# A two-layer retention and block-attention trunk: a load behind a transpose counted later, and a rotation's last steps ranked lower

## The chip, the core and the metric

The kernel runs on one core of a Trainium2 chip. Five engines work side by side, each through its own list of instructions in order: TensorE (PE, matrix products), VectorE (DVE), ScalarE (ACT), GpSimd (POOL) and SyncE (SP). In this kernel SP issues nearly all DMAs. The metric is the time of one execution on the device in microseconds (us), lower is better.

## What is computed

The reference, cut to its body. `D_MODEL` is 1024, there are 256 positions, two layers, four retention heads and four attention heads of 128 columns each.

```python
for i in range(DEPTH):
    h = rms_norm(x, norm_g[i])
    proj = h @ w_in[i]
    rq, rk, rv, rz, mq, mk, mv, mz = jnp.split(proj, cuts, axis=-1)
    r_out = retention(rotary(heads(rq, RET_HEADS), pos), rotary(heads(rk, RET_HEADS), pos),
                      heads(rv, RET_HEADS), ret_norm_g[i])
    r_out = jax.nn.silu(rz.astype(f32)) * r_out
    q_m = rms_norm(heads(mq, MOBA_HEADS), q_norm_g[i])
    k_m = rms_norm(heads(mk, MOBA_HEADS), k_norm_g[i])
    m_out = moba(q_m, k_m, heads(mv, MOBA_HEADS), rel_bias)
    m_out = jax.nn.silu(mz.astype(f32)) * m_out
    y = jnp.concatenate([r_out, m_out], axis=-1).astype(x.dtype) @ w_out[i]
    x = x + y
    gate = jax.nn.sigmoid((rms_norm(x) @ w_ple_gate[i]).astype(f32))
    e = rms_norm(p[i] @ w_ple[i], ple_norm_g[i]).astype(f32)
    x = x + (gate * e).astype(x.dtype)
```

With 256 positions there is one attention block, so `moba` is causal softmax attention with a bias by distance. `retention` is a decayed product of queries and keys times values, in two chunks of 128, with a norm per head. `rotary` turns pairs of columns: `x1*cos - x2*sin` and `x1*sin + x2*cos`.

## The kernel before

**Products in three parts.** Each float32 matrix is split into a high part (a copy rounded to the type that PE multiplies) and a low part (the rest). A product is three matmuls into one PSUM bank: high times high, high times low, low times high (`mm3`, lines 358, 359 and 360). The 256 positions are two halves m of 128 rows.

**Weights.** They come in 96 pieces of 0.5 MB (`Stage`). Each piece is one load by SP into a buffer `wst` (line 314, eight buffers), a rounding copy on ACT into `wh` (line 319), and a subtraction on DVE into `wl` (line 321). In the second half of each layer some pieces go to buffers lent by other tiles and are called T, V, PS or G in the rows. I count the pieces from 1 in the order of their loads. PE uses one piece for twelve matmuls as a rule.

**Stages of a layer.** The input projection runs by groups of 512 columns: MQ, MK, RQ, RK, MZ, MV, RV, RZ (M for attention, R for retention; queries, keys, values and gate). Then follow the output projection, a small product for the per-layer embedding, and its gate. Each result in PSUM (`acc`, four banks) is read by a chain of small steps on the other engines:

- MQ and MK: a norm (`qk_norm`).
- RQ and RK: the rotation (`rope`), for each m a product with cosines (line 732, into `tmp`), a product with sines (line 734, into `tok`; after it the bank is free), and their sum (line 737).
- All of these, the softmax probabilities and the inputs of the next product then have to be turned, since PE needs them the other way round. ACT copies the 16-bit halves apart (`halves`, line 520, into `u`), SP issues a DMA transpose (`turned`, line 530, `w<-u`), and DVE copies the halves together again (line 539, two copies each).

Two short groups of PE work stand between the projections: the attention scores (line 820) and, later, the probabilities times values (line 831), and the same for retention (lines 882 and 831).

**What sets the order.** The program is put in order while it is written, by a planner in the kernel (`Flow`). PE's work is written out by hand. Every other step is part of a chain (a Python generator) that asks for an engine and a cost (`ask`). Each time PE's clock moves on, the planner takes the engine that can start first, and among the chains that can start on it then, the one with the smallest key; a key is about the time by which PE needs the chain. `lay` advances the clocks. For DMAs the planner keeps one more clock, `dma`: a load adds 2.5 us per MB (3.3 at first), a transpose 1.4 us. `can` holds back a DMA whose start lies far ahead of that clock, and a load that isn't urgent if a transpose would soon be ready. On the chip nothing of these clocks is left: the engines keep the order and wait on semaphores.

The key of a rotation is PE's clock plus 4 (RQ) or 2 (RK) when its bank is full, and holds for the whole chain, from the first product to the last turned copy. The key of a piece of weights is its due time less 7, so it moves up as PE nears it.

Of the kernel before, what the change touches and what calls it, by code (L numbers as in the profile page):

```python
# [60 lines left out]
class Chain:  # L61
# [3 lines left out]
    def __init__(self, gen, key, at):  # L65
        self.gen, self.key, self.ready, self.done, self.on = gen, key, at, False, None
        self.next()
# [14 lines left out]
class Flow:  # L82
# [4 lines left out]
    def __init__(self, slots):  # L87
        self.clock = {PE: 0.0, ACT: 3.0, DVE: 1.0, POOL: 1.0, SP: 0.7}
        self.dma = 0.0
        self.live = []  # L90
        self.free_at = {k: [0.0] * n for k, n in slots.items()}
        self.lent, self.lending = [], False
        self.loaded = 0.0
        self.end = 0.0

    def begin(self, gen, key, at=None):
# [53 lines left out]
    def lay(self, start, c):  # L150
        eng, cost, take, after, mb = c.want
        for s in take:
            t = min(self.free_at[s])
            self.free_at[s].remove(t)
            self.got = None
            for i, (at, names) in enumerate(self.lent):
                if s == "w" and at == t:
                    self.got = self.lent.pop(i)[1]
                    break
        if eng == POOL and start - self.clock[POOL] > 1.5:  # L160
            cost += 0.9
        self.end = self.clock[eng] = start + cost
        c.ready, c.on = self.end, eng
        if mb is not None:
            rate = 3.3 if self.dma < 11 else 2.5
            self.dma = max(self.dma, start + (1.3 if mb else 1.0)) + (rate * mb if mb else 1.4)
            c.ready = self.dma + (0.9 if mb else 0.65)
            if mb:
                self.loaded = start
            else:  # L170
                c.ready += 0.75 * max(0.0, self.loaded + 2.6 - start)
        c.next()
        if c.done:
            self.live.remove(c)
# [57 lines left out]
def ask(eng, cost, take=(), after=(), mb=None):  # L232
    return eng, cost, take, after, mb
# [3 lines left out]
def tile_hybrid_trunk(ctx: ExitStack, tc: tile.TileContext, first, rest, x, pT, ple_g, rel_bias,  # L237
# [278 lines left out]
    def halves(src, name):  # L516

        yield ask(ACT, 0.95, take=("u16",))
        u = tok_p.tile([P, 2, GW], U16, name="u16", bufs=U_BUFS)
        nc.scalar.copy(u, src.bitcast(U16).rearrange("p (n t) -> p t n", t=2))  # L520
        if name:
            flow.free(name)
        return u
# [151 lines left out]
    def layer(l, aT):  # L675
        last = l == DEPTH - 1
        T, TC, V, G, VC, GC = {}, {}, {}, {}, {}, {}
# [7 lines left out]
        def to_heads(name, m, u, scale=None):  # L685

            def raw():
                if name not in T:
                    T[name] = big.tile([P, H, S], F32, name="T")
                return T[name].bitcast(U16).rearrange("p h (k t) -> p t h k", t=2)[:, :, :, m * P:(m + 1) * P]  # L690
            yield from turned(u, raw, () if m else ("T",))
            if scale is not None:
                dst = T[name][:, :, m * P:(m + 1) * P]
                yield ask(ACT, 0.64)
                nc.scalar.activation(dst, dst, AF.Copy, scale=scale)
# [26 lines left out]
        def rope(g, m, ps):  # L722


            src = ps.rearrange("p (h a d) -> p h a d", h=H, a=2)
            cos, sin = (rot[:, m, j].rearrange("p (a d) -> p a d", a=2)[:, None].to_broadcast([P, H, 2, DH // 2])
                        for j in range(2))
            yield ask(DVE, 0.605, take=("tmp", "tok"), after=(L_ROT,))
            t = tmp_p.tile([P, GW], F32, name="tmp")
            o = tok_p.tile([P, GW], F32, name="tok")  # L730
            tv, ov = (v.rearrange("p (h a d) -> p h a d", h=H, a=2) for v in (t, o))
            nc.vector.tensor_tensor(tv, src, cos, op=ALU.mult)
            yield ask(DVE, 0.605)
            nc.vector.tensor_tensor(ov, src[:, :, ::-1], sin, op=ALU.mult)  # L734
            flow.free("acc")
            yield ask(DVE, 0.605)
            nc.vector.tensor_tensor(o, o, t, op=ALU.add)
            flow.free("tmp")
            u = yield from halves(o, "tok")
            yield from to_heads(g, m, u)  # L740
# [19 lines left out]
        def after_proj(g, m, ps):  # L760
            fn, slack = {MQ: (qk_norm, -3 if l else 2), MK: (qk_norm, -3 if l else 0), RQ: (rope, 4), RK: (rope, 2), MZ: (gate, 4),
                         MV: (value, 1), RV: (value, -4), RZ: (gate, -4)}[g]
            c = flow.begin(fn(g, m, ps), flow.soon(slack))
            {MV: VC, RV: VC, MZ: GC, RZ: GC}.get(g, TC)[g, m] = c
            if g == RZ:
                YC[m, 0] = made(yT, m, 0, flow.begin(ret_gate(m), flow.soon(-5)))
# [397 lines left out]
```

## Time and profile before

| | |
|---|---|
| time, median of three runs | 308.04 us (307.85, 308.04, 311.3) |
| the profiled execution, first to last instruction (span) | 305.8 us |
| DVE busy | 251.1 us (82%) |
| ACT busy | 210.1 us (69%) |
| POOL busy | 33.8 us (11%) |
| the 96 subtractions of line 321, of which 83 into `wl` | 99.6 us for the 83, 1218 ns each |
| the 40 + 32 + 12 copies of line 539 | 16.3 + 12.6 + 4.8 us, about 455 ns each |
| mean granted TensorE clock | 0.997 |

The profiled execution has its span, and no time of its own beside it: the median of the runs lies 2.2 us above the span, for what lies before the first and after the last instruction. In the rows, "128x512" is partitions by elements, "x4" a count, and in brackets stands how long the engine was idle before the row and what ended that. Rows of a timeline begin with start and duration in us; instructions of one engine overlap a little, so the pace is taken from start to start.

### The profile page before, as it was taken

To read this page: it belongs to the slowest core of one execution; us is meant where nothing else is said; L and a number is where in the kernel's file an instruction comes from. 1 tells how busy PE (TensorE), PEld (TensorE's weight loads), DVE (VectorE), ACT (ScalarE), POOL (GpSimd) and SP (SyncE) were. 2 spreads that over 40 slices of the span, in tenths; PEclk is the share of its full clock that TensorE was granted. 3 is DMA by queue.
4 is the path that set the end of the run, shared out by engine and by line. 5 is a ranking of instruction groups with operands and counts; after the bars stand their busy time and mean duration, and the time that the engine had idled before them with its cause. 6 is when DMAs were issued, how large, how long until landed. Compare 5 with 4: busy or idle time off the path is not lost.

```text
span 305.8 us, 4251 instructions
## 1 busy us (share of the span) xinstructions
PE 298.7 (98%) x1393; PEld 248.8 (81%) x1393; DVE 251.1 (82%) x463; ACT 210.1 (69%) x359; POOL 33.8 (11%) x44
## 2 busy tenths in 40 slices
PE   8999999979999999999999999999999999999994
PEld 4888888868888888888888888888888888888884
DVE  4986899799787798799998578999868779959832
ACT  4976949885455975997694795797445678499211
POOL 6005200000002200121002220000000130012000
PEclk9999999999999999999999999999999999999998
DMA  7998999999579868795879669678976956833011
GB/s 252 406 408 302 286 290 278 274 273 353 220 145 375 270 175 275 166 230 223 214 230 266 219 171 270 146 172 190 383 287 135 339 195 192 241 75 64 0 71 69
DMA packets 61773, 69.76 MB, mean 228 GB/s; under 512 B 46260, under 2 KB 47032, under 8 KB 61624
## 3 DMA queue, kind: packets, MB, share of 16 engines
q1 hardware_dynamic: 61712, 69.50, 76.5%
q8 instruction: 11, 0.18, 0.2%
q14 instruction: 10, 0.08, 0.1%
q0 software_dynamic: 32, 0.01, 0.0%
q10 hardware_dynamic: 8, 0.00, 0.0%
HBM read 57.42 MB, written 1.05 MB: 191 GB/s over the span
## 4 chain that ended last, share of the span: by engine, by line
PE 89%; DVE 5%; DMA 2%; issue 1%; ACT 1%; DVEq 0%; ACTq 0%
PE acc L359 25%; PE acc L360 25%; PE acc L358 25%; PE acc L454 4%; PE mix L831 4%; DVE wl L321 2%; DMA w<-u 2%; PE mix L273 1%; PE mix L651 1%; PE mix L649 1%; PE mix L650 1%; PE mix L882 1%; ACT tok L802 1%; PE mix L820 1%; DVE tok L734 1%
## 5 line engine op out<-in xcount | busy, mean ns | idle before, releaser
L359 PE MATMUL acc<-wl,a 128*128 128x512 f32 (+1 forms) x332 | 127.6, 384 | 1.6 <-DVE wl L321 1.6
L358 PE MATMUL acc<-wh,a 128*128 128x512 f32 (+1 forms) x332 | 128.4, 387 | 0.0
L360 PE MATMUL acc<-wh,a 128*128 128x512 f32 (+1 forms) x332 | 127.5, 384 | 0.0
L321 DVE TENSOR_TENSOR wl<-wst,wh 128x1024 fp32r<-128x1024 f32 x83 | 99.6, 1218 | 12.2 <-ACT wh L319 12.0
L319 ACT CAST wh<-wst 128x1024 fp32r<-128x1024 f32 x83 | 86.1, 1057 | 26.7 <-PE acc L360 13.6
L359 PEld LDWEIGHTS acc<-wl,a 128*128 128x128 f32 x332 | 62.4, 188 | 14.2 <-DVE wl L321 2.0
L360 PEld LDWEIGHTS acc<-wh,a 128*128 128x128 f32 x332 | 62.4, 188 | 12.3
L358 PEld LDWEIGHTS acc<-wh,a 128*128 128x128 f32 x332 | 62.4, 188 | 12.0
L520 ACT COPY u<-tok 128x1024 uint16<-128x1024 uint16 x30 | 31.2, 1050 | 8.3 <-DVE tok L849 5.8
L572 POOL TENSOR_TENSOR ro<-rs_t,neghalf 128x4 f32<-128x4 f32 x4 | 7.7, 1913 | 130.3 <-DVE rs_t L570 130.3
L556 ACT CAST a<-tmp 128x512 fp32r<-128x512 f32 x20 | 12.4, 620 | 10.3 <-DVE tmp L539 5.7
L539 DVE COPY tmp<-w 128x512 uint16<-128x512 uint16 x40 | 16.3, 454 | 3.1 <-DMA w<-u 3.0
L520 ACT COPY u<-x_t 128x1024 uint16<-128x1024 uint16 x12 | 12.5, 1045 | 6.5 <-DVE x_t L984 4.3
L539 DVE COPY T<-w 128x512 uint16<-128x512 uint16 x32 | 12.6, 454 | 2.2 <-DMA w<-u 2.2
L558 DVE TENSOR_TENSOR a<-tmp,a 128x512 fp32r<-128x512 f32 x20 | 13.6, 682 | 0.0
L713 POOL TENSOR_TENSOR qr<-qms,neghalf 128x4 f32<-128x4 f32 x8 | 9.5, 1196 | 28.6 <-DVE qms L711 28.6
L831 PEld LDWEIGHTS mix<-V,PS 128*128 128x128 f32 x96 | 11.3, 192 | 0.3
L831 PE MATMUL mix<-V,PS 128*128 128x128 f32 x96 | 11.4, 275 | 0.0
L1031 ACT ACTIVATE tmp<-acc,hr 128x512 f32<-128x512 f32 (+1 forms) x7 | 4.6, 657 | 9.6 <-PE acc L360 9.6
L707 ACT ACTIVATE tmp<-acc 128x128 f32<-128x128 f32 x32 | 8.4, 286 | 3.3 <-PE acc L360 3.2
L572 POOL TENSOR_TENSOR r<-rs_t,neghalf 128x1 f32<-128x1 f32 x4 | 5.2, 1292 | 49.2 <-DVE rs_t L570 49.2
L319 ACT CAST T<-wst 128x1024 fp32r<-128x1024 f32 x8 | 8.4, 1052 | 3.1 <-PE acc L359 1.5
(120 smaller groups left out, 368.4 us busy)
## 6 DMA issues: line engine op xcount, KB each, us to landing
wst<-in_w_in SPq DMA_DIRECT2D x60, 512.0 KB, 5.9
wst<-in_w_out SPq DMA_DIRECT2D x16, 512.0 KB, 7.6
wst<-in_w_gate SPq DMA_DIRECT2D x16, 512.0 KB, 4.3
wst<-in_w_ple SPq DMA_DIRECT2D x4, 512.0 KB, 5.9
wst<-in_rest SPq DMA_DIRECT2D x4, 384.0 KB, 6.8
a<-in_rest SPq DMA_DIRECT2D x3, 384.0 KB, 4.7
x_t<-in_x SPq DMA_DIRECT2D x1, 1024.0 KB, 10.5
gb<-in_ple_g SPq DMA_DIRECT2D x2, 512.0 KB, 8.4
```

What stands on the lines that cost most here:

```text
L319: nc.scalar.copy(hi, s)
L321: nc.vector.tensor_tensor(lo, s, hi.bitcast(F32), op=ALU.subtract)
L358: nc.tensor.matmul(ps, ah, wh[:, cols], start=start, stop=False)
L359: nc.tensor.matmul(ps, ah, wl[:, cols], start=False, stop=False)
L360: nc.tensor.matmul(ps, al, wh[:, cols], start=False, stop=stop)
L454: nc.tensor.matmul(ps[m], (a0.lo if which[0] == "lo" else a0.hi)[:, k, m * P:(m + 1) * P], w, start=start and i == 0, stop=stop and i == 2)
L520: nc.scalar.copy(u, src.bitcast(U16).rearrange("p (n t) -> p t n", t=2))
L539: nc.vector.tensor_copy(v, w[:, t].rearrange("p (h b) k -> p h (b k)", h=v.shape[1]))
L556: nc.scalar.copy(h, src)
L558: nc.vector.tensor_tensor(a.lo[:, k0:k0 + 4, m * P:(m + 1) * P], src, h.bitcast(F32), op=ALU.subtract)
L572: nc.gpsimd.tensor_tensor(dst, t[:, :n], neghalf[:, :n], op=ALU.pow)
L831: nc.tensor.matmul(ps[:, h * DH:(h + 1) * DH], lhs(h, m, b), v[:, b, h * DH:(h + 1) * DH], start=b == 0, stop=b == m)
```

## The change

Two edits, both in the planner's bookkeeping; no instruction is added, removed or altered.

1. `lay` remembers whether the last DMA was a transpose (`TURN` is 0, so `mb` is 0 for one). The first load behind a transpose moves the planner's DMA clock on by another 1.0 us.
2. In `rope`, when the product with sines has been placed and the bank is given back, the key of the chain goes up by 4.0, so that the sum, the copy of the halves, the transpose and the last copies rank lower from then on.

```diff
-        self.loaded = 0.0
+        self.loaded, self.after_turn = 0.0, False
@@ def lay
             rate = 3.3 if self.dma < 11 else 2.5
+            if mb and self.after_turn:
+                self.dma += 1.0
+            self.after_turn = not mb
             self.dma = max(self.dma, start + (1.3 if mb else 1.0)) + (rate * mb if mb else 1.4)
@@ def rope
             nc.vector.tensor_tensor(ov, src[:, :, ::-1], sin, op=ALU.mult)
             flow.free("acc")
+            TC[g, m].key += 4.0
             yield ask(DVE, 0.605)
             nc.vector.tensor_tensor(o, o, t, op=ALU.add)
```

Every line below the edits has a number higher by 3 or 4 (line 321 is 324, line 737 is 741). PE's own order stays but for one thing: in layer 0 the sixteen matmuls of the scores (line 820) stand six matmuls later. On the other engines many rows move. Three places matter below.

DVE in layer 0, in the rotation of RK. The rows before (`tok_680` and `tok_726` are the two rotated halves, `PS` the turned probabilities, `wl_580` is piece 16, `wl_693` piece 17, the first of MV):

```order
L732 TENSOR_TENSOR tmp_679<-acc_513,cst_112 128x512
L321 TENSOR_TENSOR wl_580<-wst_534,wh_579 128x1024
L734 TENSOR_TENSOR tok_680<-acc_513,cst_112 128x512
L539 COPY PS_588<-w16_658 128x4x128 x2
L539 COPY PS_588<-w16_677 128x2x256 x2
L737 TENSOR_TENSOR tok_680<-tok_680,tmp_679 128x512
L732 TENSOR_TENSOR tmp_725<-acc_523,cst_112 128x512
L734 TENSOR_TENSOR tok_726<-acc_523,cst_112 128x512
L539 COPY PS_588<-w16_699 128x2x256 x2
L737 TENSOR_TENSOR tok_726<-tok_726,tmp_725 128x512
L321 TENSOR_TENSOR wl_693<-wst_547,wh_692 128x1024
L321 TENSOR_TENSOR wl_706<-wst_559,wh_705 128x1024
```

The same place now (`wl_588` is piece 16, `wl_615` piece 17, `wl_701` piece 18):

```order
L735 TENSOR_TENSOR tmp_675<-acc_511,cst_112 128x512
L324 TENSOR_TENSOR wl_588<-wst_549,wh_587 128x1024
L737 TENSOR_TENSOR tok_676<-acc_511,cst_112 128x512
L542 COPY PS_594<-w16_662 128x4x128 x2
L735 TENSOR_TENSOR tmp_705<-acc_523,cst_112 128x512
L737 TENSOR_TENSOR tok_706<-acc_523,cst_112 128x512
L542 COPY PS_594<-w16_683 128x2x256 x2
L324 TENSOR_TENSOR wl_615<-wst_560,wh_614 128x1024
L741 TENSOR_TENSOR tok_676<-tok_676,tmp_675 128x512
L542 COPY PS_594<-w16_703 128x2x256 x2
L741 TENSOR_TENSOR tok_706<-tok_706,tmp_705 128x512
L324 TENSOR_TENSOR wl_701<-wst_572,wh_700 128x1024
```

Piece 17 now stands ahead of both sums and of the last pair of copies; the reads of the banks stand earlier, the sums later.

SP's queue at the same place. Before (`w16_592` and `w16_614` are the two halves of RQ, the next three transposes the probabilities):

```order
L530 DMA_TRANSPOSE w16_592<-u16_574 128x8x128
L314 DMA wst_601<-in_w_in 128x1024
L530 DMA_TRANSPOSE w16_614<-u16_605 128x8x128
L314 DMA wst_627<-in_w_in 128x1024
L314 DMA wst_641<-in_w_in 128x1024
L530 DMA_TRANSPOSE w16_658<-u16_644 128x8x128
L530 DMA_TRANSPOSE w16_677<-u16_666 128x8x128
L530 DMA_TRANSPOSE w16_699<-u16_687 128x8x128
L314 DMA wst_709<-in_w_in 128x1024
L314 DMA wst_723<-in_w_in 128x1024
```

And now:

```order
L533 DMA_TRANSPOSE w16_608<-u16_598 128x8x128
L533 DMA_TRANSPOSE w16_621<-u16_604 128x8x128
L317 DMA wst_631<-in_w_in 128x1024
L533 DMA_TRANSPOSE w16_662<-u16_651 128x8x128
L533 DMA_TRANSPOSE w16_683<-u16_673 128x8x128
L533 DMA_TRANSPOSE w16_703<-u16_693 128x8x128
L317 DMA wst_718<-in_w_in 128x1024
```

One load instead of three stands ahead of the probabilities' transposes; the loads of pieces 21 and 22 come later. From here to the end of the program every transpose has two to five loads fewer ahead of it than before (counted in SP's list: 71 of the 96 ahead of layer 1's probabilities before, 66 now).

SP's queue in layer 1 around the probabilities, now (`w16_2101`, `w16_2119` and `w16_2140`; `wst_2155` is piece 67, the first of MV in layer 1):

```order
L317 DMA wst_2027<-in_w_in 128x1024
L533 DMA_TRANSPOSE w16_2054<-u16_2043 128x8x128
L533 DMA_TRANSPOSE w16_2073<-u16_2062 128x8x128
L533 DMA_TRANSPOSE w16_2101<-u16_2088 128x8x128
L533 DMA_TRANSPOSE w16_2119<-u16_2108 128x8x128
L533 DMA_TRANSPOSE w16_2140<-u16_2125 128x8x128
L317 DMA wst_2155<-in_w_in 128x1024
L317 DMA wst_2170<-in_w_in 128x1024
```

Before, pieces 67 to 71 had been loaded by then. The other place of this kind is the end of layer 1's projection: the second of the two loads of `w_ple` (piece 88) now stands behind a transpose, where before four loads of `w_gate` stood ahead of it.

## The prediction

> **What bounds the kernel now.** I read the page first, then the busy time by stages, PE's waits, and the timelines of PE and DVE where PE waits. The page:
>
> ```profile
> span 305.8 us, 4251 instructions
> ...
> PE 298.7 (98%) x1393; PEld 248.8 (81%) x1393; DVE 251.1 (82%) x463; ACT 210.1 (69%) x359; POOL 33.8 (11%) x44
> ```
>
> PE is idle for 7.1 us of the span. The busy times by stretch (length, then each engine's busy time with its count, granted clock, DMA share, GB/s) and PE's waits say where:
>
> ```profile
> core 0: us, PE busy (x) PEld busy (x) DVE busy (x) ACT busy (x) POOL busy (x), PEclk, DMA share, GB/s
> 38.00:65.00 27.00, 25.44 (x117) 20.99 (x116) 24.75 (x40) 21.03 (x35) 0.00 (x0) 1.00 1.07 285
> 65.00:191.00 126.00, 126.00 (x585) 105.45 (x586) 108.15 (x199) 89.86 (x152) 14.87 (x12) 1.00 0.82 238
> 191.00:222.00 31.00, 31.00 (x143) 25.91 (x142) 29.18 (x44) 22.75 (x38) 0.00 (x0) 1.00 0.83 225
> 222.00:301.00 79.00, 79.00 (x400) 67.45 (x399) 59.13 (x124) 47.11 (x72) 7.15 (x6) 1.00 0.52 156
> ```
>
> ```profile
> PE acc L359 <- DVE wl L321: 1.6, 1, 1.6
> PE mix L273 <- DVE neghalf L278: 1.2, 1, 1.2
> ```
>
> From 65 to 301 us PE never rests. What is left is the start, the tail after the last matmul, and one wait of 1.56 us between 38 and 65, for a low part of weights. The change alters neither start nor tail, so it can win that one wait and no more; anything else it does can only cost. The wait, in PE's timeline:
>
> ```profile
> 62.87 0.39 PE L358 MATMUL acc<-wh,a 128*128 128x512 f32 x1
> 64.82 0.50 PE L359 MATMUL acc<-wl,a 128*128 128x512 f32 x1 [1.56 <-DVE wl L321]
> 65.16 0.39 PE L360 MATMUL acc<-wh,a 128*128 128x512 f32 x1
> 65.39 0.40 PE L358 MATMUL acc<-wh,a 128*128 128x512 f32 x1
> ```
>
> PE's pace is 0.23 us from start to start (65.16 to 65.39). From 62.87 to 65.39 three steps take 2.52 us instead of 0.68, so the wait costs 1.84 us with the restart. DVE's timeline says why:
>
> ```profile
> 38.60 2.35 DVE L321 TENSOR_TENSOR wl<-wst,wh 128x1024 fp32r<-128x1024 f32 x2
> 40.87 1.61 DVE L539 COPY T<-w 128x512 uint16<-128x512 uint16 x4
> 42.37 0.67 DVE L734 TENSOR_TENSOR tok<-acc,cst 128x512 f32<-128x512 f32 x1
> ...
> 47.88 0.68 DVE L795 TENSOR_TENSOR tok<-mix,tb 128x512 f32<-128x512 f32 x1
> 48.59 0.69 DVE L799 TENSOR_REDUCE nm<-tok 128x4 f32<-128x512 f32 x1
> 49.20 0.68 DVE L795 TENSOR_TENSOR tok<-mix,tb 128x512 f32<-128x512 f32 x1
> ...
> 51.04 0.80 DVE L539 COPY T<-w 128x512 uint16<-128x512 uint16 x2 [0.44 <-DMA w<-u]
> ...
> 55.39 0.81 DVE L539 COPY T<-w 128x512 uint16<-128x512 uint16 x2 [1.13 <-DMA w<-u]
> ...
> 58.85 1.75 DVE L539 COPY PS<-w 128x512 uint16<-128x512 uint16 x4 [0.36 <-DMA w<-u]
> 60.48 0.68 DVE L737 TENSOR_TENSOR tok<-tok,tmp 128x512 f32<-128x512 f32 x1
> 61.07 0.69 DVE L732 TENSOR_TENSOR tmp<-acc,cst 128x512 f32<-128x512 f32 x1
> 61.67 0.69 DVE L734 TENSOR_TENSOR tok<-acc,cst 128x512 f32<-128x512 f32 x1
> 62.27 0.79 DVE L539 COPY PS<-w 128x512 uint16<-128x512 uint16 x2
> ...
> 63.55 3.49 DVE L321 TENSOR_TENSOR wl<-wst,wh 128x1024 fp32r<-128x1024 f32 x3
> ```
>
> Piece 17 is the first of the three at 63.55. ACT had the rounded copies of pieces 17 to 20 done long before (56.16, below), so it was DVE's order alone that kept PE: RK's rotation and the probabilities' copies stood ahead, and DVE had idled 0.44 + 1.13 + 0.36 = 1.93 us for transposes on the way.
>
> **The change, part by part.** Both edits act only through the order, and they meet in DVE's list. I add up that list from 40.87 us, where the old and the new order part (pieces 11 and 12 are done in both). Paces from the rows: a subtraction 1.14 (38.60 to 40.87 for two), two copies 0.75 (40.87 to 42.37 for four), a step of the rotation 0.60 (60.48, 61.07, 61.67, 62.27), a bias 0.71 with its maximum 0.61 behind it.
>
> - RQ's rotation and pieces 13 to 15: sines 0.60, four copies 1.50, cosines 0.60, piece 13 1.14, sines 0.60, two sums 1.20, pieces 14 and 15 2.27. Sum 7.91, to 48.78.
> - Scores: two biases with maxima 2.64, two copies 0.75, a bias 0.60, two copies 0.75, a maximum 0.61. Sum 5.35, to 54.13.
> - RK's rotation: cosines 0.60, piece 16 1.14, sines 0.60, two copies 0.75, cosines 0.60, sines 0.60, two copies 0.75. Sum 5.04, to 59.17.
> - Piece 17 starts at 59.17 and is done 1.22 later, at 60.39.
>
> PE wants it at 62.87 + 0.23 = 63.10. The margin is 2.7 us if DVE waits for no transpose, and 0.8 if it waits the 1.93 us of before. Neither sum of RK is worse off: the first starts at 60.31, the second at 61.66 behind two copies, against 60.48 and 62.95 (0.68 after 62.27) before, so the later transposes of RK lose nothing on DVE. Piece 18 follows the second sum at 62.26, is done at 63.5, and is wanted twelve matmuls after piece 17, at 65.8.
>
> The moved transposes decide which margin holds. The rows for them: ACT's copies, SP's issues, and the time to landing of transposes and of loads in this stretch.
>
> ```profile
> 53.14 1.05 ACT L520 COPY u<-tok 128x1024 uint16<-128x1024 uint16 x1
> ...
> 56.16 3.90 ACT L319 CAST wh<-wst 128x1024 fp32r<-128x1024 f32 x4
> ```
>
> ```profile
> 52.70 6.42 SPq L530 DMA_TRANSPOSE w<-u  x3
> ```
>
> ```profile
> DMA to landing us min/median/max: 3.1/5.0/6.4
> ```
>
> ```profile
> DMA to landing us min/median/max: 4.7/6.1/8.3
> ```
>
> The last transpose whose copies stand ahead of piece 17 is that of the second block of probabilities. Its halves were ready at 54.19 (53.14 + 1.05); the scores start 0.9 us later now (48.78 for 47.88), so 55.1. With 3.1 to 6.4 us to landing (the first of the two landing lines) it lands between 58.2 and 61.5, and its copies are due at 58.42. So piece 17 is done between 60.4 and 63.5: margin 2.7 to -0.4. I take the lower half, since one load instead of three stands ahead of it in the queue. The term is -1.84 us, with -1.4 at the bad end.
>
> What the edits take for it: loads. From here on each transpose has two to five loads fewer ahead of it, so the pieces' margins shrink. In layer 0 and in most of layer 1 the subtractions of the pieces are done so early that this costs nothing; the cover is a lead of several pieces at 2.7 us (twelve matmuls) each. It is thin at two places in layer 1, both where a load now stands behind a transpose:
>
> ```profile
> 197.73 5.38 SPq L530 DMA_TRANSPOSE w<-u  x3
> 203.16 0.57 SPq L314 DMA_DIRECT2D wst<-in_w_in  x1
> ```
>
> ```profile
> wst<-in_w_in SPq DMA_DIRECT2D x1, 512.0 KB, 3.6
> ```
>
> ```profile
> 211.61 0.39 PE L359 MATMUL acc<-wl,a 128*128 128x512 f32 x1
> ```
>
> Piece 67 takes the spot of the load at 203.16 (asked for alone, it landed after 3.6 us): 206.8, plus a rounding copy of 1.05 and a subtraction of 1.22, is 209.1. PE first reads it at 211.61. Margin 2.5: no cost.
>
> ```profile
> 255.83 0.53 SPq L314 DMA_DIRECT2D wst<-in_w_gate  x1
> ```
>
> ```profile
> wst<-in_w_gate SPq DMA_DIRECT2D x1, 512.0 KB, 3.8
> ```
>
> ```profile
> 261.57 0.68 DVE L558 TENSOR_TENSOR a<-tmp,a 128x512 fp32r<-128x512 f32 x1
> ```
>
> ```profile
> 263.37 0.39 PE L360 MATMUL acc<-V,a 128*128 128x512 f32 x1
> ```
>
> Piece 88 takes the spot of the load at 255.83 (3.8 us to landing): 259.6. Its copy (1.05) and subtraction (1.14) now stand on ACT and DVE ahead of the low part of the retention output (line 558), which so starts at 261.8 and ends at 262.5. PE reads that at 263.37. Margin 0.9, against 1.1 before: no cost, but little cover.
>
> Sum: -1.84 us on a span of 305.8, or 308.04 - 1.84 = 306.2 us on the median.
>
> [...] In the two landing lines transposes need 5.0 us and loads 6.1 in the median, so no transpose is slow here, though these lines don't show what a load behind one pays. [...]
>
> **The rivals.**
>
> *The wait stays in layer 0.* The probabilities' transposes are late and DVE stands idle ahead of piece 17. For: DVE already waited three times there. Against: the margin holds with all of the 1.93 us, and the slowest landing misses by 0.4. It needs waits of 2.7 + 1.84 = 4.5 us to keep the whole wait: 308.0. A part of it gives 306.6 to 307.9.
>
> *A new wait at the retention output of layer 1.* Piece 88 lands after 6.1 us, the median of the loads between 40 and 60 us, instead of 3.8. Then 2.3 - 0.9 = 1.4 us come back: 307.6. Against: the queue is emptier there (DMA share 0.52 after 222 us, 1.07 in the stretch of the 6.1).
>
> *Slower: a new wait for piece 67.* It decides from a landing at 209.3 (206.8 + 2.5), and the kernel is slower than before from 211.1. With the transposes as slow as in layer 0 (6.42 us for three instead of 5.38) and the load as slow as the slowest there (8.3 instead of 3.6), it lands 5.7 us later: a wait of 3.2 us, 309.4. For: SP holds the load back behind transposes that wait for ACT. Against: DMA share 0.83 there. [...] The 1.56 us wait of this trace left the clock at 1.00, and no run here shows a longer one.
>
> **How the numbers follow.** The wait goes and none comes: 0.66 (306.2, within 0.5). It stays in whole or part: 0.12. The retention output: 0.12. Slower by piece 67 or a place that I hold to be covered: 0.09. Something else: 0.01. The range 305.6 to 308.4 holds the forecast with the runs' scatter (307.85 to 308.04 for two of three) and the first two rivals; what is left out is the slower one and the rest. Faster by over 2% would be under 301.9, which needs 6.2 of the 7.1 us that PE is idle, start and tail included: 0.01. Slower by over 2% is above 314.2: 0.02. Within 2%: 0.97; about 2% is also what a measurement of this kernel can tell from no change.
>
> **What would show it.** Right: PE's waits hold only the 1.2 us at the start; PE is busy for 27.00 us of 38 to 65; piece 17's subtraction ends before 62; the span is near 303.9. Wrong: a PE wait on `wl` at 60 to 66 (first rival), on `a` near 261 (second), on `wl` near 210 (third; 1.84 us earlier than in this trace). It would also be wrong if PE waited where I counted no cost, for a bank or a turned tile.

## The result, and the profile after

The changed kernel takes 306.12 us in the median of 16 runs, the kernel before 307.98 us in the median of 16. The ratio is 0.993, with a 95% interval from 0.9911 to 0.9949: a gain of 0.5 to 0.9%, clear of no change and well under 2%. The forecast was 306.2 us, by way of one wait that goes away. The ratios here and below are taken over fast runs alone (a run over 1.5% above the fastest of its kernel, as one of e3 at 311.21 us, counts as slow), so they are not the quotients of the medians, which are over all runs.

The page of the changed kernel:

```profile
span 304.2 us, 4215 instructions
...
PE 298.1 (98%) x1393; PEld 247.7 (81%) x1393; DVE 250.4 (82%) x463; ACT 209.1 (69%) x359; POOL 30.0 (10%) x44
```

Its busy times by stretch (columns as before) and its list of PE's waits:

```profile
38.00:65.00 27.00, 27.00 (x126) 22.57 (x124) 25.67 (x42) 20.78 (x35) 0.00 (x0) 1.00 0.92 233
65.00:191.00 126.00, 126.00 (x590) 105.66 (x589) 108.97 (x201) 90.16 (x152) 12.17 (x12) 1.00 0.78 233
191.00:222.00 31.00, 31.00 (x139) 25.73 (x138) 23.83 (x38) 20.14 (x35) 0.00 (x0) 1.00 0.80 224
222.00:299.00 77.00, 77.00 (x390) 65.72 (x389) 62.17 (x127) 48.87 (x75) 7.10 (x6) 1.00 0.60 187
```

```profile
PE mix L276 <- DVE neghalf L281: 1.2, 1, 1.2
PE acc L457 <- ACT a L417: 0.6, 1, 0.6
```

PE is busy for all of 38 to 299 us. The 25.44 us of the stretch 38 to 65 have become 27.00. The second wait, 0.6 us, is new in this profile and does not belong to the change: line 457 is the first product, in the first 17 us, where PE waits for inputs that arrive from memory (ACT waited 1.29 us for a load, `a<-in_rest`, just ahead of the row that released PE), and a second profile of the same kernel (e9 below) does not have it. It makes the gain in the span (305.8 to 304.2) look smaller than it is. To leave the start out I measure from the first matmul of line 358 (now 361) to the end of the last matmul, in PE's timeline of the kernel before and of the changed one:

```profile
16.71 0.39 PE L358 MATMUL acc<-wh,a 128*128 128x512 f32 x1
...
301.19 0.28 PE L360 MATMUL acc<-wh,a 128*128 128x256 f32 x1
```

```profile
17.03 0.39 PE L361 MATMUL acc<-wh,a 128*128 128x512 f32 x1
...
63.41 0.39 PE L362 MATMUL acc<-wl,a 128*128 128x512 f32 x1
...
299.65 0.28 PE L363 MATMUL acc<-wh,a 128*128 128x256 f32 x1
```

Before, that stretch is 301.19 + 0.28 - 16.71 = 284.76 us, now 299.65 + 0.28 - 17.03 = 282.90 us. The difference is 1.86 us, where the sum had 1.84. I call this stretch "the planned part" below. It is the cleanest measure of every experiment, though of one execution each; two profiles of the same program (changed and e9, e7 and e10) differ by 0.1 us at most. The planned part starts at another time in each profile (16.71, 17.03), which has to be taken off when times of two profiles are compared. The row at 63.41 is PE's first read of piece 17's low part. DVE's timeline of the changed kernel shows where that came from:

```profile
41.19 0.68 DVE L737 TENSOR_TENSOR tok<-acc,cst 128x512 f32<-128x512 f32 x1
...
52.62 0.81 DVE L542 COPY T<-w 128x512 uint16<-128x512 uint16 x2 [0.96 <-DMA w<-u]
...
59.37 0.83 DVE L542 COPY PS<-w 128x512 uint16<-128x512 uint16 x2
60.04 1.24 DVE L324 TENSOR_TENSOR wl<-wst,wh 128x1024 fp32r<-128x1024 f32 x1
61.17 0.72 DVE L741 TENSOR_TENSOR tok<-tok,tmp 128x512 f32<-128x512 f32 x1
61.77 0.83 DVE L542 COPY PS<-w 128x512 uint16<-128x512 uint16 x2
```

Piece 17 is made at 60.04 + 1.24 = 61.28, ahead of both sums of RK and of the last copies, 2.1 us before PE reads it. DVE waited for a transpose only once, 0.96 us, instead of three times and 1.93 us. (The row at 41.19 is the first of the list that the prediction adds up.) How long DMAs of each kind took from issue to landing says why. This line is for the transposes between 45 and 62 us of the changed kernel (minimum, median, maximum), where the kernel before had 3.1, 5.0 and 6.4:

```profile
DMA to landing us min/median/max: 3.1/3.8/4.9
```

### The profile page after: what moved, and what is told of

It is laid out like the page before. It is cut to its first block, busy times and chain, and to the rows that moved or that the text cites. A ratio compares the mean times of both kernels' runs of the same rounds, so it can differ in the third digit from the quotient of the medians.

```text
span 304.2 us, 4215 instructions
## 1 busy us (share of the span) xinstructions
PE 298.1 (98%) x1393; PEld 247.7 (81%) x1393; DVE 250.4 (82%) x463; ACT 209.1 (69%) x359; POOL 30.0 (10%) x44
## 4 chain that ended last, share of the span: by engine, by line
PE 96%; DMA 2%; ACT 0%; DVE 0%; SPq 0%; issue 0%
PE acc L361 27%; PE acc L363 27%; PE acc L362 27%; PE mix L835 4%; PE acc L457 3%; PE mix L824 2%; DMA a<-in_rest 2%; PE mix L652 1%; PE mix L654 1%; PE mix L653 1%; PE mix L886 1%; PE mix L887 1%; ACT wh L409 0%; DVE x_t L1068 0%; DVE tmp L1066 0%; ACT a L417 0%
## 5 line engine op out<-in xcount | busy, mean ns | idle before, releaser
L575 POOL TENSOR_TENSOR ro<-rs_t,neghalf 128x4 f32<-128x4 f32 x4 | 6.7, 1685 | 129.9 <-DVE rs_t L573 129.9
L457 PE MATMUL acc<-wh,a 128*128 128x512 f32 x32 | 9.1, 401 | 0.6 <-ACT a L417 0.6
L361 PE MATMUL acc<-T,a 128*128 128x512 f32 x24 | 9.3, 389 | 0.0
L363 PE MATMUL acc<-T,a 128*128 128x512 f32 x24 | 9.3, 389 | 0.0
```

The lines of the kernel that those rows point to most:

```text
L361: nc.tensor.matmul(ps, ah, wh[:, cols], start=start, stop=False)
L363: nc.tensor.matmul(ps, al, wh[:, cols], start=False, stop=stop)
L457: nc.tensor.matmul(ps[m], (a0.lo if which[0] == "lo" else a0.hi)[:, k, m * P:(m + 1) * P], w, start=start and i == 0, stop=stop and i == 2)
```

## The experiments

Each table row gives the median of the runs, the ratio to the kernel before with its 95% interval, and the planned part from the profile's PE timeline. The kernel before was run beside each group of experiments: its median was 308.07 us beside e1 to e4, 307.88 beside e5 to e7, and 307.85 beside e8 to e10.

| kernel | time, us | ratio | planned part, us |
|---|---|---|---|
| before | 307.98 | | 284.76 |
| changed | 306.12 | 0.993 (0.9911 to 0.9949) | 282.90 |
| e1 clock only | 305.69 | 0.9893 (0.985 to 0.9937) | 283.22 |
| e2 key only | 306.30 | 0.9917 (0.9887 to 0.9947) | 283.64 |
| e3 piece 17 alone | 306.57 | 0.992 (0.9882 to 0.9958) | 283.56 |
| e4 piece 17 late again | 306.10 | 0.9914 (0.9878 to 0.9951) | 282.94 |
| e5 clock 2.0 | 324.78 | 1.0551 (1.0502 to 1.0601) | 301.98 |
| e6 loads held back | 307.13 | 0.9979 (0.9951 to 1.0006) | 284.54 |
| e7 key 8.0 | 305.46 | 0.9913 (0.9883 to 0.9944) | 282.90 |
| e8 clock 1.2 | 310.03 | 1.0069 (1.0037 to 1.0101) | 286.49 |
| e9 changed, once more | 306.20 | 0.9932 (0.9905 to 0.9958) | 282.99 |
| e10 key 8.0, once more | 305.60 | 0.9912 (0.9881 to 0.9944) | 282.92 |

The intervals of the changed kernel and of e1 to e4 overlap. The times show that each of these gains something; how the gain divides is read from the planned parts.

### Which of the two edits removes the wait?

e1 leaves the second edit out, e2 the first:

```diff
@@ e1, against the changed kernel
-            TC[g, m].key += 4.0
@@ e2, against the changed kernel
-                self.dma += 1.0
+                self.dma += 0.0
```

> Only the first edit (the planner's DMA clock), without the lower rank of the rotation's rest. On DVE piece 17 then stands behind both sums of RK but ahead of the probabilities' last two copies. Theory A (DVE's list in layer 0 is all that kept PE, and either edit brings piece 17 in time): the changed kernel had piece 17 made at 61.3 for a read at 63.4, and here two sums of 0.6 us stand ahead of it in addition, so it is made near 62.5, 0.9 us in time: no wait on wl near 63, span 303.9 +- 0.4, time near 306.1. Theory B (the lower rank of the sums is what brings it): the wait comes back in large part, 0.8 to 1.6 us on wl near 63, time 307.1 to 308.

> Only the second edit (the rotation's rest ranks lower once its bank is read). Piece 17 then stands ahead of both sums and of the probabilities' last copies, and 21 pieces are loaded ahead of the probabilities' transposes (22 before, 20 with both edits). Theory A: the second block of probabilities is copied at about 59.5 as before, two steps of the rotation (1.2) and piece 17 (1.2) follow, made near 62.0, wanted at 63.1: no wait, time near 306.1. In layer 1 the 71 loads ahead of the probabilities' transposes are back, so the pieces of MV there are made earlier than with both edits: the smallest margin between 205 and 222 us is over 1.5 us instead of 0.5. Theory C (fewer loads ahead of the transposes, so the first edit, are what frees DVE): DVE waits for transposes as before, over 1.5 us between 48 and 60, and part of the wait stays: 306.8 to 308.

In e1, transposes between 45 and 62 us land after 3.3 us in the median (5.0 before, 3.8 with both edits). DVE's timeline has piece 17 here:

```profile
60.32 1.21 DVE L324 TENSOR_TENSOR wl<-wst,wh 128x1024 fp32r<-128x1024 f32 x1
```

It is made at 61.53, though both sums stand ahead of it, and PE reads it at 62.52: no wait. Theory A holds, with a margin of 1.0 us where it had 0.9 (all times lie earlier than it said, as the planned part starts at 16.14 instead of 17.03). The planned part is 0.3 us longer than with both edits, for a small wait at 152 us on an input of layer 1, which the changed kernel doesn't have.

e2 shows the other half. Its DVE and PE timelines:

```profile
54.47 0.81 DVE L542 COPY T<-w 128x512 uint16<-128x512 uint16 x2 [2.12 <-DMA w<-u]
...
62.44 1.23 DVE L324 TENSOR_TENSOR wl<-wst,wh 128x1024 fp32r<-128x1024 f32 x1
```

```profile
63.18 0.39 PE L361 MATMUL acc<-wh,a 128*128 128x512 f32 x1
63.72 0.50 PE L362 MATMUL acc<-wl,a 128*128 128x512 f32 x1
64.05 0.39 PE L363 MATMUL acc<-wh,a 128*128 128x512 f32 x1
```

DVE waits 2.12 us for a transpose, as theory C said; piece 17 is made at 63.67, and PE, which would have read it at 63.41, reads it at 63.72. With the restart that is 0.4 us (0.87 us for two steps of 0.23), and a second wait of the same kind costs 0.26 us at 66.7. So A's "no wait" was wrong here: the place in the list alone gives 284.76 - 283.64 = 1.12 of the 1.86 us. C's time was wrong too: 306.30 us were measured, where it had 306.8 to 308. The smallest margin of a piece between 205 and 222 us is 3.9 us, where it is 0.5 with both edits: that part of A's expectation held.

### Is it the place of piece 17, and nothing else?

e3 is the kernel before with a lower key for that one subtraction; e4 is the changed kernel with a higher one.

```diff
@@ e3, against the kernel before (in e4, against the changed kernel: - 5.0)
             nc.scalar.copy(hi, s)
+            if 2 * self.i + c == 20: self.chains[c].key = lambda: due(20) - 11.0
             yield ask(DVE, 1.135)
```

> The kernel before, neither edit, with a lower key for the one subtraction of piece 17 (due time less 11 instead of less 7). It then stands ahead of RK's first sum, the last copies of the probabilities and the whole second rotation; PE's order and nearly all else are as before. Theory D (piece 17 was merely one too late in the list; its place is enough): made at 61.7 instead of 64.76, no wait, time near 306.1. Theory A with the second bank (the two products of the second rotation have to be early as well, since they give back the bank that MV needs three matmuls after piece 17): the product with sines is pushed from 62.35 to about 64.2, PE wants the bank at 63.5, so a new wait of about 0.7 us with 0.3 for the restart, now on the product with sines of line 734: time near 307.1. If the order of the scores on PE (six matmuls later with the change) were the cause of the gain, this kernel would stay at 308.

> The changed kernel, both edits, with a higher key for the one subtraction of piece 17 (due time less 5): it stands behind both sums and behind the last copies of the probabilities again, as in the kernel before; the loads ahead of the transposes stay as changed. Theory A (order of the list plus DVE's waits for transposes, each good for its sum): from the changed kernel's trace, 60.04 plus two sums (1.2) plus two copies (0.75, their transpose landed at 60.5, so no wait) puts its start at 62.0 and its end at 63.2, against a read at 63.4: just in time or a wait of up to 0.4 us, time 306.1 to 306.8. Theory B (the place of piece 17 is the whole gain): the wait of 1.56 us is back, time near 308.

DVE and PE of e3:

```profile
59.92 1.21 DVE L321 TENSOR_TENSOR wl<-wst,wh 128x1024 fp32r<-128x1024 f32 x1
...
62.92 0.68 DVE L734 TENSOR_TENSOR tok<-acc,cst 128x512 f32<-128x512 f32 x1
```

```profile
62.99 0.39 PE L360 MATMUL acc<-wh,a 128*128 128x512 f32 x1
63.76 0.47 PE L358 MATMUL acc<-wh,a 128*128 128x512 f32 x1 [0.38 <-DVE tok L734]
```

Piece 17 is made at 61.13 and PE doesn't wait for it. It waits for the bank instead: the product with sines, pushed back behind piece 17, ends at 63.60, and PE wanted the bank at 63.22. Theory D falls; the place and kind are those that theory A expected, the size is smaller: 0.66 us of the planned part (283.56 against 282.90) where 1.0 was expected. That is what the second edit does in the order: it lets the sums give way, so that both the piece and the reads of the banks can be early. PE's own order is as before in e2 and e3, which gain 1.12 and 1.20 us, and what they lack is in the waits that are left; so the scores that stand six matmuls later in the changed kernel have no visible part in the gain.

In e4 the piece stands behind both sums and the last copies, as before the change:

```profile
60.87 0.81 DVE L542 COPY PS<-w 128x512 uint16<-128x512 uint16 x2
61.55 3.50 DVE L324 TENSOR_TENSOR wl<-wst,wh 128x1024 fp32r<-128x1024 f32 x3
```

Piece 17 is the first of the three at 61.55; it is made at 62.78, PE reads it at 63.34. No wait, 282.94 us. With the loads out of the transposes' way the old order of DVE is good enough, by 0.56 us in this profile. That is thin: DVE waited 0.65 us for a transpose here, but 0.96 and 1.39 in the two profiles of the changed kernel, and 1.39 would use up the 0.56. Theory B falls. Both edits work on the same sum: the earlier transposes alone take away the whole wait (e4), the place in the list alone 1.12 of 1.86 us (e2), and together they leave 2.1 us to spare (1.7 in e9).

### Are loads ahead of the transposes what made DVE wait?

e6 is the kernel before, with pieces 20 and later held back until the probabilities' transposes are issued:

```diff
-                    self.chains[c] = flow.begin(self.gen(c), lambda c=c: due(2 * self.i + c) - 7, 0.0)
+                    self.chains[c] = flow.begin(self.gen(c), lambda c=c: due(2 * self.i + c) - 7, 56.0 if 2 * self.i + c >= 23 else 0.0)
```

> The kernel before, neither edit, with the loads of pieces 20 and later held back in the planner until the probabilities' transposes have been issued (20, 21 and 22 move behind them). Piece 17 stays behind both sums and the last copies of the probabilities on DVE. Theory F (the loads ahead of the transposes made DVE wait; taking them away is worth those waits): DVE's waits for transposes between 48 and 60 us fall from 1.93 to under 0.6 us, piece 17 starts near 62.0 instead of 63.55 and is made at 63.2 for a read at 63.1: a wait of 0 to 0.5 us, time 306.1 to 306.7. Theory B (the place of piece 17 in the list is the gain; transposes are late because ACT's copies are): DVE's waits stay over 1.2 us, PE's wait is over 0.8 us, time 307 to 308.

The transposes between 45 and 62 us of e6, then its DVE and PE rows:

```profile
DMA to landing us min/median/max: 3.0/3.1/5.3
```

```profile
52.17 0.80 DVE L539 COPY T<-w 128x512 uint16<-128x512 uint16 x2 [1.17 <-DMA w<-u]
...
62.77 3.48 DVE L321 TENSOR_TENSOR wl<-wst,wh 128x1024 fp32r<-128x1024 f32 x3
```

```profile
64.03 0.50 PE L359 MATMUL acc<-wl,a 128*128 128x512 f32 x1 [0.75 <-DVE wl L321]
```

The median landing falls from 5.0 to 3.1 us. One transpose shows it more sharply, the first of the probabilities. With two loads issued between it and the transpose ahead of it, it landed after 6.1 us (the kernel before, and e3, whose queue is the same); with one, after 3.8 (the changed kernel) and 4.3 (e9); with none, after 3.0 (e6). So the loads ahead are what made it slow. DVE's waits fall from 1.93 to 1.17 us (all of it now at the first transpose, the one with 5.3 us, which five loads still precede); but e3, with SP's queue as before, has 1.35, so this sum scatters by some 0.6 us from one profile to the next. Piece 17 starts 0.78 us earlier than before, and PE's wait shrinks by as much, 1.56 to 0.75. By these numbers the run lies at the edge of theory B (over 1.2, over 0.8, 307 to 308 us), and F was too bold. What speaks for F's mechanism is the landing, since B held ACT's copies to be what is late. The time says less (its interval holds no change), because a new wait near 165 us, on an input of layer 1, takes 0.55 us back.

### How far from the edge does the change stand?

The first edit's 1.0 us was varied to 2.0 and 1.2, the second's 4.0 to 8.0:

```diff
-                self.dma += 1.0
+                self.dma += 2.0
@@ e8
-                self.dma += 1.0
+                self.dma += 1.2
@@ e7 and e10
-            TC[g, m].key += 4.0
+            TC[g, m].key += 8.0
```

> Both edits, with 2.0 us instead of 1.0 for the load behind a transpose. Still fewer loads stand ahead of each transpose; in layer 1 piece 67, the first of MV, now stands behind the transposes of the probabilities and of RK, where with 1.0 it stood ahead of RK's. Theory A (a late piece costs what it is late, and the rival about piece 67 is real, only one step away): by the changed kernel's trace the load behind RK's transposes is issued at 210.4 and lands at 215.4; copy and subtraction make the piece at 217.7, PE wants it at 210.1: a wait of about 7.6 us on wl near 210, time near 314 (312 to 316), slower than before. Layer 0 stays without a wait (piece 18 made near 58). Theory E (a later load finds emptier queues and transposes end earlier, so little is lost): wait under 2 us, time 306 to 308. [...]

> Both edits, with 8.0 instead of 4.0 added to the rotation's key. Piece 17 then stands ahead of all copies of the probabilities, both sums stand later still; the loads ahead of each transpose are up to two more than with 4.0. Theory A: nothing waits for the sums for a long while, piece 17 is made near 60.5 for a read at 63.1 to 63.4, no wait in layer 0; time near 306.1, no difference from the changed kernel. Theory G (RK's turned halves are needed soon, so pushing the sums further back makes a new wait): a wait at the retention's scores or on the first weights of the next group, 0.5 us or more, time over 306.6.

> Both edits, with 1.2 us instead of 1.0 for the load behind a transpose. One piece less stands ahead of RK's transposes in layer 1: piece 69 is now the first behind them, where with 1.0 it is piece 70. Theory A (the lead is used up piece by piece; a rule read from the changed kernel's trace): the first load behind RK's transposes is made into a low part at 217.7, whatever its number; PE wants piece 70 at 218.2 (margin 0.5, as measured with 1.0) and piece 69 at 215.5, so a wait of about 2.2 us on wl near 215.5 and a time near 308.4 (307.6 to 309), about that of the kernel before. Theory E (moving one load by one place is made good by an emptier queue): no wait over 0.5 us there, time 306.1 to 306.6.

> The changed kernel itself once more, beside the other two. Theory A: no wait behind the first product; from the first matmul of line 361 to the end of the last one 282.9 us as before in its profile, where the kernel before needed 284.8; what differs between profiles of kernels without a wait is when the first product ends (16.1 to 17.1 us after the start), which no edit touches. Time 305.4 to 306.5.

> The changed kernel with 8.0 instead of 4.0 for the rotation's rest, once more. Theory A: no wait in either, so the same time as the changed kernel within 0.3 us, and 282.9 us from the first matmul of line 361 to the end of the last. Theory H (the 0.7 us by which its median lay lower is real): lower again by 0.5 us or more in the same company.

The wait list of PE in e5:

```profile
PE acc L362 <- DVE wl L324: 4.8, 6, 1.2
PE acc L361 <- ACT wh L322: 4.0, 4, 1.7
PE acc L362 <- DVE T L324: 1.9, 1, 1.9
PE mix L276 <- DVE neghalf L281: 1.2, 1, 1.2
PE acc L361 <- ACT T L322: 0.9, 1, 0.9
PE acc L363 <- DVE a L561: 0.3, 1, 0.3
```

Slower, by 5.5%, and piece 67 is among the late ones, but the expectation of one wait of 7.6 us and 314 us in all was wrong. There are thirteen waits behind the start, from 118 us on, for rounded copies as well as low parts, the longest of them 1.9 us; PE idles 11.9 us in them. By the time PE came to piece 67 it had been held up so often that only 2.7 us were left to wait there. Theory E is off by more, with its 306 to 308 us. I had moved one piece in my head; the edit withholds loads in both layers, and the lead that covered them was gone everywhere.

e8 moves the edge by a fifth of a microsecond. Its waits, and the place that was expected, on DVE and PE:

```profile
PE acc L362 <- DVE wl L324: 1.5, 2, 0.8
...
PE acc L363 <- DVE a L561: 0.3, 1, 0.3
```

```profile
216.30 1.23 DVE L324 TENSOR_TENSOR wl<-wst,wh 128x1024 fp32r<-128x1024 f32 x1 [1.24 <-ACT wh L322]
```

```profile
217.59 0.50 PE L362 MATMUL acc<-wl,a 128*128 128x512 f32 x1 [0.77 <-DVE wl L324]
```

Piece 69, now behind RK's transposes, is made at 217.53, and PE waits for it. The rule had 217.7, but the planned part starts 0.77 us earlier here (16.26) than in the changed kernel, so the rule was 0.6 us too early. PE waits 0.77 instead of 2.2 us because PE itself was late already: near 168 us it had waited 0.19 and 0.77 us for piece 54, as much as at the expected place. It waits once more, 0.30 us, for the low part of the retention output at 264 us. All in all 3.6 us of the planned part are lost (286.49 against 282.9), and the kernel is slower than before by 0.4 to 1.0%: 310.03 us, where 307.6 to 309 were expected. Theory E falls, theory A holds in kind and place, and its sum again had a place too few.

e7 and e10 (8.0 for the rotation's rest) have no wait behind the start: 282.90 and 282.92 us, the same planned part as the changed kernel in both its profiles (282.90, 282.99). Theory G falls. Their medians lie 0.6 us lower, beside e9 (305.60 against 306.20) and in the earlier group (305.46, where the changed kernel was not run), as theory H said; but the intervals of the ratios overlap (0.9881 to 0.9944 and 0.9905 to 0.9958), so the difference isn't settled. The profiles don't show where it would come from. One candidate, not tried, is that the changed kernel's thin margins (below) fail in some executions and not in the profiled ones; e10 has over 3 us for every piece behind 50 us, though its retention output has only 0.3 too. Nor is 8.0 shown to be the best version: e1, with the clock alone, has 305.69 us and the lowest ratio.

## Why the prediction was right

**The place and the term.** PE's one wait was the whole prize, and it went: 1.86 us against 1.84 (1.77 in e9). DVE's list was summed to 60.39 us for piece 17 without waits and 62.3 with the old 1.93. Measured: 61.28 with a wait of 0.96. That looks good to 0.1 us (60.39 + 0.96 = 61.35), but the list starts at 41.19 in this profile and at 40.87 in the prediction. From there to the end of piece 17 are 20.09 us, 19.13 without the wait, where the sum had 19.52: it was 0.4 us too long, spread over all its parts, and the later start hid that. That the medians of the runs fell by 1.86 us as well may be in part chance (see the clock below).

**The transposes.** They were taken to come in the lower half of 58.2 to 61.5, for want of loads ahead. The copies of the second block ran at 59.37 without a wait. e6 and the landings beside it show that the reason was the right one: fewer loads ahead, sooner landed.

**The two edits "meet in DVE's list".** So they do, but the prediction didn't say how the gain divides. e1, e2 and e4 do: the clock alone takes away the whole wait (and loses 0.3 us at another place), the key alone gives 1.1 of 1.9 us, and with the clock the old place of piece 17 is good enough.

**The cover.** Here the prediction's steps were wrong, and that this cost nothing is luck. The rows are from the changed kernel, SP, ACT, DVE and PE in layer 1:

```profile
207.70 2.62 SPq L533 DMA_TRANSPOSE w<-u  x2
210.38 4.15 SPq L317 DMA_DIRECT2D wst<-in_w_in  x7
```

```profile
215.45 1.05 ACT L322 CAST wh<-wst 128x1024 fp32r<-128x1024 f32 x1 [3.77 <-DMA wst<-in_w_in]
```

```profile
206.76 1.22 DVE L324 TENSOR_TENSOR wl<-wst,wh 128x1024 fp32r<-128x1024 f32 x1 [1.23 <-ACT wh L322]
...
216.53 1.23 DVE L324 TENSOR_TENSOR wl<-wst,wh 128x1024 fp32r<-128x1024 f32 x1 [2.03 <-ACT wh L322]
...
260.86 0.68 DVE L561 TENSOR_TENSOR a<-tmp,a 128x512 fp32r<-128x512 f32 x1
```

```profile
218.22 0.39 PE L362 MATMUL acc<-wl,a 128*128 128x512 f32 x1
...
261.83 0.39 PE L363 MATMUL acc<-V,a 128*128 128x512 f32 x1
```

- "Margin 2.5" for piece 67. It is made at 207.98, where the sum had 209.1; PE reads it at 210.06, where the sum had 211.61: 2.1. The two errors cancel. And the prediction stopped at the first load behind the probabilities' transposes. RK's transposes follow, SP stands 5 us for them (202.6 to 207.7), and piece 70 is the first load behind those (210.38). It is made at 217.76 for a read at 218.22: a margin of 0.5, the thinnest of all pieces, at a place that was held to be covered. e8 took one load more away and this cover failed.
- "Margin 0.9" for the retention output. The low part ends at 261.54, PE reads it at 261.83: 0.3. The load of piece 88 took the 3.8 us that were assumed. What was missed is PE's own gain: PE comes here 1.54 us sooner than before (263.37 to 261.83), the input's chain only 0.71 us (261.57 to 260.86, and that with piece 88's subtraction now ahead of it).

Both sums set an input's new time against PE's old one. With the 1.84 us taken off, the prediction's own numbers leave 0.7 us for piece 67 and -0.9 for the retention output, which is a new wait and the second rival. It didn't come because both inputs were about 1 us earlier than the sums had them (207.98 for 209.1, and 261.54 for 262.5).

**The rivals.** None came true at the change's own numbers. All three exist: the wait in layer 0 stays in part in e2 and e6, the retention output waits in e8, and the slower kernel by late loads is e5 and, with another piece, e8. The change stands 0.2 us of a planner's constant from the slower one, at piece 69, which the prediction hadn't looked at.

## What to carry to other kernels

Where one engine is busy for all but one wait, the wait with its restart is the whole prize, and the sum of the late engine's list from the last common point gives the new time well enough (here 19.5 us summed for 19.1 measured, waits for transposes left out); then every margin that the change thins has to be taken at the new time of the winner, which comes sooner by what it won. A planner's constant that moves loads behind other DMAs spends a lead that no wait shows: list the margins of all pieces before and after, not of those that the diff makes conspicuous. A measured price was no guide to the constant here: at one place of the changed kernel a load behind transposes landed up to 2 us later than one behind a load, and the planner with 2.0 us is 18.7 us slower than with 1.0, since the loads that it held back were late themselves (thirteen waits of PE in e5, 11.9 us).

## What the hardware showed that was not expected

**PE's clock fell behind waits of under 2 us.** In e5 the granted clock (the number behind the busy times) fell twice. Busy times of e5 by stretch:

```profile
213.00:216.00 3.00, 1.37 (x6) 0.59 (x5) 2.32 (x4) 3.00 (x4) 0.00 (x0) 1.00 1.01 170
216.00:220.00 4.00, 4.00 (x13) 3.10 (x12) 2.92 (x6) 1.18 (x2) 0.00 (x0) 0.61 0.91 181
222.00:226.00 4.00, 1.28 (x5) 0.51 (x3) 3.13 (x6) 3.25 (x4) 0.00 (x0) 1.00 0.87 303
227.00:230.40 3.40, 3.40 (x9) 2.60 (x9) 3.05 (x4) 2.65 (x4) 0.00 (x0) 0.51 1.03 417
```

Ahead of the first fall PE idled twice, 0.87 and 0.77 us, with one matmul between; ahead of the second 1.71 and 1.02 us. About 1 us after each restart the pace of the matmuls went from 0.23 to 0.43 us for some 3 us, and back; eight matmuls at 0.2 us more are 1.6 us each time. Over the two stretches the granted clock was 0.61 and 0.51; the longest single gap ahead of a fall was 1.71 us. Two similar pairs of gaps near 138 us (0.86 and 1.92) and 199 us (0.94 and 0.75) in the same run left the clock at 1.00, as the one gap of 1.56 us did in the profile of the kernel before. So the length of the gaps does not tell when the clock falls, and no run here shows what does.

The kernel before may pay for such falls too, in executions that weren't profiled. Beside the experiments it was run 65 times. In 46 of these the mean granted clock was 0.996 or more and the median time 307.7 us; in 19 it was 0.986 to 0.994, and the median 309.7. The versions that keep PE from waiting behind the start for more than 0.03 us (changed, e1, e4, e7, e9 and e10) were run 54 times, never below 0.996; e8, with two waits of 0.77 us, was below it in 3 of 12, e3 and e6 (0.38 and 0.75 us) in 1 of 12 each, e2 (0.15 us) in none of 10. So the wait of 1.56 us seems to cost a fall of the clock in about three executions of ten, and the change takes that away as well. This is argued from the counts: no trace of such an execution was kept. Beside e9, the executions of the kernel before with 0.996 or more have a median of 307.65 us against e9's 306.20. That is 1.4 us, less than the 1.77 of the planned parts; the scatter of e9's runs (305.1 to 307.6) leaves open whether the rest means anything.

**A load behind transposes.** In the changed kernel the transpose issued at 209.0 landed after 3.1 us, at 212.1, and the first load behind it, issued at 210.4, landed after 5.1:

```profile
wst<-in_w_in SPq DMA_DIRECT2D x1, 512.0 KB, 5.1
```

That is 3.3 us behind the transpose; the next loads followed 1.3 to 1.95 us apart (ACT's copies start as they land: 215.45, 217.40, 219.15, 220.46). Here the load behind a transpose comes 1.4 to 2 us later than one behind a load, more than the first edit's 1.0. But it isn't so everywhere. In the kernel before, the load at 203.16 landed after 3.6 us, 1.8 behind its transpose (issued at 201.87, landed after 3.1), which is the pace between loads; there no other load was issued until it had landed, while six more followed the one at 210.38 at once. So the premise of the first edit holds at some places, and whether it is the transpose or the loads that follow that make the 3.3 us, no run here separates. At both places the transpose itself, 0.25 MB, landed sooner after its issue (3.1 us) than the load of 0.5 MB behind it (5.1 and 3.6).
